# Split weight tiles kept in DRAM, and a depthwise convolution as diagonal matrix products

## The chip, the core and the metric

The kernel runs on one core of one Trainium2 chip. A core has five engines that run side by side, each from its own queue in order: TensorE (matrix products, "PE" in the profile, with "PEld" for loading its stationary operand), VectorE ("DVE"), ScalarE ("ACT"), GpSimd ("POOL") and SyncE ("SP", which here only issues transfers). Transfers between DRAM and on-chip memory run on 16 DMA engines. The metric is the device time of one execution in microseconds (us). Before the change it is 3492.43 us, the median of three runs (3483.12 to 3494.14).

## What is computed

The reference is one layer of a streaming encoder over 1024 tokens of 1024 channels in float32. Cut to what matters here:

```python
h = adaln(x, shift1, scale1)                  # layer norm, shifted and scaled by the condition c
p = h @ w_in                                  # 1024 -> 2816 columns
p_conv, p_rw = p[..., :1024], p[..., 1024:]

u = p_conv[..., :512] * sigmoid(p_conv[..., 512:])
u = causal_depthwise_conv(u, conv_w) + conv_b # 31 taps, one filter for each of 512 channels
y_conv = silu(layer_norm(u, conv_ln_g, conv_ln_b))

y_rw = rwkv7(p_rw)                            # recurrence over tokens, 8 heads of 64
y1 = concat([y_conv, y_rw]) @ w_out
x = layer_norm(ALPHA * x + gate1 * y1)

h2 = adaln(x, shift2, scale2)
q = h2 @ peer_wq                              # 1024 -> 2048 columns
# q against 2 x 128 keys for each of 8 heads, top 16, softmax -> 16 experts and gates for each head
# each of 16384 experts: gelu(h2 . u_e) * gate * v_e, summed over the chosen ones
return layer_norm(ALPHA * x + gate2 * y2)
```

## The kernel before

The kernel has a front end and a dense stage. The front end covers everything up to the choice of experts. The dense stage then runs all 16384 experts for 640 of the 1024 tokens as matrix products on TensorE, while the other 384 tokens gather their experts' rows by GpSimd transfers and use VectorE. The change lies in the front end alone.

Large products are made of float32 operands split in two: a high part in the reduced type float32r (`hi`) and the remainder (`lo`), so that a product is three float32r matmuls (hi x hi, hi x lo, lo x hi). `load_split` (L158) does this for a tile of weights, 128 contraction rows x 8 x 128 columns, 0.5 MB: it loads it raw by SP (L155, tile `wraw`, three buffers), ScalarE copies it to `whi` (L161), GpSimd subtracts to make `wlo` (L163), two buffers each. `proj` (L166) then issues 24 matmuls (L173) into one bank of the PSUM pool `psum`, whose tag `mm` (L145) has three buffers. Tiles of the 22 of `w_in` are loaded for each half of the tokens, the 8 of `w_out` and the 16 of `wq` for each of four blocks of 256 tokens: 44 + 32 + 64 = 140 calls.

The tokens go through in two halves of 512:

- `inproj(0)` (L262) runs first and alone: norm, transposition to channels, the condition's matrix-vector products on VectorE (`cond_some`, L234), all `w_in` tiles, and the streams for the recurrence, which it stores in DRAM (`AR_d`, `BK_d`, `v_d`, `bv_d`, `gt_d`). Its `glu` (L323) fills `ubuf`, 4 groups of 128 channels x (30 + 512) tokens, and appends `conv(0)` to the list `slow`.
- The recurrence follows in 16 chunks of 64 tokens: `solve` (L576) inverts each chunk's triangular system by a chain of small TensorE products and VectorE steps, `pass_state` (L654) carries the state. Between their matmuls `fill` (L553) is called, some 80 times for each chunk. It takes steps of the generators in `side` (`inproj(1)`, then `post` for each block of 256 tokens) and at every fourth call one step of the first generator in `slow` (the convolution, then `choose` and `gate_matrix`).
- `conv` (L436) handles 4 groups of 128 channels. In each, 18 taps are accumulated on VectorE in `cacc` (L443, L449), 13 on ScalarE and GpSimd: ScalarE scales a window into `ctap` (L453), GpSimd adds it to `cpool` (L454), and VectorE adds both sums (L457). Then come two sums over the channels by a matrix of ones (L460, L468) and the norm. `inproj(1)` drains `conv(0)` before its own `glu` overwrites `ubuf`, and the main loop drains `conv(1)` before chunk 8.
- `post` (L734): `w_out`, residual and norm, transposition, `wq`, keys and top 16. `choose` (L834) picks the 16 of 16 x 16 candidates, `gate_matrix` (L909) builds for each token block the matrix of gates over all experts out of one-hot tiles (`oa` L928, `ob` L932 to L944, products L946, `stage` L947) and stores it in DRAM as `G_d` (L949), 2 MB at a time from one buffer.

Semaphores and the order on each engine are made by the scheduler of the framework, which takes the order of the program's text as priority and moves an instruction ahead where its own model of time finds an engine free. Each engine then runs its queue in the order so fixed.

Of the kernel before, what the change touches and what calls it, by code (L numbers as in the profile page):

```python
# [10 lines left out]
F32 = mybir.dt.float32  # L11
F32R = mybir.dt.float32r
# [3 lines left out]
AF = mybir.ActivationFunctionType  # L16
OP = mybir.AluOpType
# [6 lines left out]
KD = 8  # L24
CW = 512
KS = 31
# [24 lines left out]
PSG, PSD = 3, 3  # L51
SLOW = 4
NTMP = 28
WRAW = 3
RUN = 4
STEPS = 4, 3
RATES = 1.0, 2.0
# [21 lines left out]
def layer_kernel(ctx, tc, x, cols, c_row, cond_w, w_in, w2a2, g2, w_out, ln_rows, wq, keys, peer_u, peer_ut, peer_v, peer_vt, out):  # L79
    nc = tc.nc  # L80
    V, A, G, T = nc.vector, nc.scalar, nc.gpsimd, nc.tensor
    ld = nc.sync.dma_start
# [3 lines left out]
    dram = ctx.enter_context(tc.tile_pool(name="dram", bufs=1, space=DRAM))  # L86
# [5 lines left out]
    def col(n, i=None):  # L92
        a, b = COFF[n]
        return colt[:, a:b] if i is None else colt[:, a + i:a + i + 1]
# [5 lines left out]
    ident = const.tile([128, 128], F32)  # L100
# [28 lines left out]
    h2_d = dt([128, D], "h2_d", 8)  # L129
    h2t_d = dram.tile([2, KD, 128, ND], F32, name="h2t_d")  # L130
    sel_d = dt([3, 128, 128], "sel_d", 8)
    G_d = dram.tile([32, 128, ND // TB, 4 * TB], F32, name="G_d")


# [2 lines left out]
    ws = fex.enter_context(tc.tile_pool(name="ws", bufs=2))  # L137
# [6 lines left out]
    def mm(w=512):  # L144
        return psum.tile([128, 512], F32, tag="mm", name="mm")[:, :w]  # L145
# [4 lines left out]
    def page(name, dt=F32, w=512):  # L150
        return pgp.tile([128, max(w, 512)], dt, tag="pg", name=name)[:, :w]

    def load_raw(src):
        raw = ws.tile([128, KD, 128], F32, name="wraw", bufs=WRAW)
        ld(raw, src)  # L155
        return raw

    def load_split(src):  # L158
        raw = load_raw(src)
        hi = ws.tile([128, KD, 128], F32R, name="whi")  # L160
        A.activation(hi, raw, AF.Copy)  # L161
        lo = ws.tile([128, KD, 128], F32R, name="wlo")
        G.tensor_sub(lo, raw, hi.bitcast(F32))  # L163
        return hi, lo

    def proj(w, act, pt):  # L166
# [95 lines left out]
    def inproj(h, ps, pg_):  # L262
# [10 lines left out]
        hi = [page("hhi", F32R) for _ in range(KD)]  # L273
        lo = [page("hlo", F32R) for _ in range(KD)]
        shift, scale = lambda k: mod[:, k:k + 1], lambda k: modp[:, k, 0:1]
        first = []
        if h == 0:

            for i in range(4):
                parts = load_x(i, tp)  # L280
                normalize(parts, parts)
                xn.append(parts)
            two = [(load_split(w_in[j]), mm()) for j in (0, 4)]
            for k in range(KD):
                cond_some((k, 8 + k), pg_)
                V.tensor_scalar_add(modp[:, k, 0:1], mod[:, 8 + k:9 + k], 1.0)
                to_channels(xn, shift, scale, hi, lo, None, (k,), m2)
                for (whi, wlo), pt in two:
                    for q, (l, r) in enumerate(((whi, hi), (whi, lo), (wlo, hi))):
                        T.matmul(pt, l[:, k, :], r[k], start=k == 0 and q == 0, stop=k == KD - 1 and q == 2)  # L290
            first = [pt for _, pt in two]
            ld(w2a2_t, w2a2)
            ld(g2_t, g2)
        else:
            for g in range(2):
                xn = []
                for i in range(2):
                    parts = load_x(4 * h + 2 * g + i, tp)
                    normalize(parts, parts)
                    xn.append(parts)  # L300
                sl = slice(256 * g, 256 * g + 256)
                to_channels(xn, shift, scale, [t[:, sl] for t in hi], [t[:, sl] for t in lo])
                yield

        def tile_of(j):
            w = load_split(w_in[j])
            pt = mm()
            yield from proj(w, (hi, lo), pt)
            return pt
# [113 lines left out]
        if h == 1:  # L423
            yield from glu()
            V.tensor_scalar_add(modp[:, :, 1], mod[:, 32:40], 1.0)
            pt = mm(128)
# [4 lines left out]


    slow, gates, gb, conv_left, psg, tail = [], [], [], [], [], []
    POOL_TAPS = 13

    def conv(h):  # L436
        acc = []
        for ct in range(4):
            wk = lambda k: colt[:, COFF["conv_w"][0] + KS * ct + k:COFF["conv_w"][0] + KS * ct + k + 1]
            win = lambda k: ubuf[:, ct, k:k + HALF]  # L440
            a, b = page("cacc"), page("cpool")
            acc.append(a)
            V.tensor_scalar(a, win(0), wk(0), col("conv_b", ct), op0=OP.mult, op1=OP.add)  # L443
            A.activation(b, win(KS - POOL_TAPS), AF.Copy, scale=wk(KS - POOL_TAPS))
            i, j = 1, KS - POOL_TAPS + 1
            while i < KS - POOL_TAPS or j < KS:
                for _ in range(2):
                    if i < KS - POOL_TAPS:
                        V.scalar_tensor_tensor(a, win(i), wk(i), a, op0=OP.mult, op1=OP.add)  # L449
                        i += 1  # L450
                if j < KS:
                    f = page("ctap")
                    A.activation(f, win(j), AF.Copy, scale=wk(j))  # L453
                    G.tensor_add(b, b, f)  # L454
                    j += 1
                yield
            V.tensor_add(a, a, b)  # L457
        pmn = mm()
        for ct in range(4):
            T.matmul(pmn, ones_m, acc[ct], start=ct == 0, stop=ct == 3)  # L460
        for ct in range(4):
            V.tensor_sub(acc[ct], acc[ct], pmn)
        yield
        pv = mm()
        for ct in range(4):
            s2 = page("s2")
            A.activation(s2, acc[ct], AF.Square)
            T.matmul(pv, ones_m, s2, start=ct == 0, stop=ct == 3)  # L468
        rs = page("crs")
        A.activation(rs, pv, AF.Sqrt, bias=eps_ln)  # L470
        V.reciprocal(rs, rs)
        yield
        for ct in range(4):
            y = acc[ct]
            V.tensor_mul(y, y, rs)
            A.activation(y, y, AF.Identity, bias=col("cln_b", ct), scale=col("cln_g", ct))
            sc_ = page("csig")
            A.activation(sc_, y, AF.Sigmoid)
            G.tensor_mul(y, y, sc_)
            ld(conv_d[h][ct], y)  # L480
            yield
        conv_left.remove(h)
# [251 lines left out]
    def post(t0, vpage):  # L734

        n, nt, tile0 = PB, PB // 128, t0 // 128
        fetch = [tile0 + t in GT for t in range(nt)]
        hp, hi = duo("ychi", F32R)
        lp, lo = duo("yclo", F32R)
        for i in range(KD // 2):  # L740
            f = page("ycf").rearrange("p (a t) -> p a t", a=2)
            if i < 2:
                c = t0 % HALF
# [7 lines left out]
        yield  # L751
        y1 = duo("y1")[1]
        for j in range(KD):
            w = load_split(w_out[j])
            pt = mm(n)
            yield from proj(w, (hi, lo), pt)
            A.activation(y1[j], pt, AF.Copy, scale=mod[:, 16 + j:17 + j])
# [8 lines left out]
        for t in range(nt):  # L766
            xt = load_x(tile0 + t, page)
            for i in range(2):
                pt = mm()
# [17 lines left out]
        hi, lo = duo("h2hi", F32R)[1], duo("h2lo", F32R)[1]  # L787
# [13 lines left out]
        for g in range(4):  # L801
            kt = pgp.tile([128, 4, 128], F32, tag="pg", name="keys")
            ld(kt, keys[:, 4 * g:4 * g + 4, :])
            qt = []
            for m in range(4):
                w = load_split(wq[4 * g + m])
                pt = mm(n)
                yield from proj(w, (hi, lo), pt)
                if m % 2 == 0:
                    qp = page("qt").rearrange("p (a t) -> p a t", a=2)  # L810
                A.activation(qp[:, m % 2, :], pt, AF.Copy)
                qt.append(qp[:, m % 2, :])
            for t in range(nt):
                ps = mm()
                for m in range(4):
                    T.matmul(ps[:, 128 * m:128 * m + 128], qt[m][:, 128 * t:128 * t + 128], kt[:, m, :],
                             start=True, stop=True)
                s = page("s12")
                A.activation(s, ps, AF.Copy)
                for m in range(4):  # L820
                    vs, ix = val[t][:, 2 * g + m // 2, m % 2], idx[t][:, 2 * g + m // 2, m % 2]
                    sm = s[:, 128 * m:128 * m + 128]
                    V.max(vs[:, 0:8], sm)  # L823
                    V.max_index(ix[:, 0:8], vs[:, 0:8], sm)  # L824
                    V.match_replace(sm, vs[:, 0:8], sm, -3.0e38)  # L825
                    V.max(vs[:, 8:16], sm)  # L826
                    V.max_index(ix[:, 8:16], vs[:, 8:16], sm)  # L827
                    yield
# [129 lines left out]
    for c in range(16):  # L958
# [16 lines left out]
        if flight:  # L975
            f = flight.pop(0)
# [40 lines left out]
    def mg(w=512):  # L1017
        return psg[0].tile([128, 512], F32, tag="mgate", name="mg", bufs=PSG)[:, :w]
# [105 lines left out]
    for g in range(32):  # L1124
# [4 lines left out]
        for e in range(4):  # L1129
# [7 lines left out]
            for bs in NBLK:  # L1137
                p = mg(NW)
                i = 0
# [12 lines left out]
        if g == 31:  # L1152
            xts = []
            for t in range(ND // 128):
                xts.append(de.tile([128, D], F32, tag="uraw" if t < 2 else "uhi" if t < 4 else "ulo", name="xres",
                                   bufs=2))
# [6 lines left out]
        for i, (blocks, c) in enumerate((b_, c) for b_ in parts for c in range(4)):  # L1163
# [3 lines left out]
            for d in range(2):  # L1167
                ds = slice(128 * d, 128 * d + 128)
                k = 2 * c + d
                for bs in blocks:  # L1170
                    p = md(bs.stop - bs.start)
# [10 lines left out]
            if g == 31 and c == 3:  # L1182
                for t in range(blocks[0].start // 128, blocks[0].stop // 128):
                    xt = xts[t]
                    for i_ in range(2):
                        pt = mg()
# [55 lines left out]
```

## Time and profile before

| what | us |
|---|---|
| median of three runs | 3492.43 |
| the profiled execution | 3490.03 |
| its span, first to last instruction | 3488.3 |
| TensorE busy | 3082.5 (88%) |
| VectorE busy | 2782.5 (80%) |
| GpSimd busy | 2134.7 (61%) |
| ScalarE busy | 1368.9 (39%) |

The page cuts the span in 40 slices of 87.2 us; a digit is the busy share of an engine in tenths (9 is 90% or more), and PEclk is the clock that TensorE was granted, in tenths of full speed. A table by stretch gives for each engine the busy time and, in brackets, the number of instructions, then the granted clock, the share of the DMA engines and GB/s. A group's row gives line, engine, operation, out<-in by the program's names, shapes and count, then busy time, the mean of one in ns, and the idle time of the engine before it with what ended it. A row by tile gives the shortest, median and longest of one in ns and the first and last start. PE instructions overlap in their pipeline, so the sum of their durations is more than the time they take together. A float32 matmul shows as two instructions, a float32r one as one; the profile writes f32 for both types.

### The profile page before, as it was taken

What the parts mean: (1) busy time and instruction counts of PE and PEld (TensorE: products, weight loads), DVE (VectorE), ACT (ScalarE), POOL (GpSimd) and SP (SyncE); (2) the same over time, 40 slices, a digit from 0 to 9 for tenths busy, and PEclk for the clock granted to TensorE, in tenths of its full rate; (3) what the DMA queues carried; (4) which work ended last, traced back from release to release, by engine and by line L of the source; (5) the groups of instructions that cost most, each with busy time, mean ns of one, the idle gap of its engine ahead of it and who ended that gap; (6) DMA issues with size and microseconds to landing.
All of it is one profiled execution on the core that took longest, in us unless ns stands there. A gap on an engine that the chain in (4) does not pass through costs nothing.

```text
span 3488.3 us, 59487 instructions
## 1 busy us (share of the span) xinstructions
PE 3082.5 (88%) x22536; PEld 2874.0 (82%) x22536; DVE 2782.5 (80%) x5776; ACT 1368.9 (39%) x2581; POOL 2134.7 (61%) x1522
## 2 busy tenths in 40 slices
PE   6965898888888766676999999999999999999997
PEld 4734566677787666576999999999999999999997
DVE  5399786897786799799777788877788877778887
ACT  4563444444554635764322222232222232222223
POOL 2446325474545366262677777687777777777773
PEclk9977788678798887787999999999999999999998
DMA  5434364333455544455799898999999989989894
GB/s 213 126 104 139 90 182 139 109 99 98 126 158 159 175 146 129 139 151 159 258 338 338 327 345 322 348 327 338 332 334 333 336 315 349 343 327 343 319 342 174
DMA packets 392223, 822.46 MB, mean 236 GB/s; under 512 B 76496, under 2 KB 209792, under 8 KB 387840
## 3 DMA queue, kind: packets, MB, share of 16 engines
q1 hardware_dynamic: 199104, 374.02, 32.5%
q0 software_dynamic: 110592, 402.70, 30.8%
q10 hardware_dynamic: 82240, 41.94, 4.3%
q8 instruction: 177, 2.90, 0.3%
q14 instruction: 110, 0.90, 0.1%
HBM read 738.84 MB, written 79.72 MB: 235 GB/s over the span
## 4 chain that ended last, share of the span: by engine, by line
PE 55%; DVE 12%; DMA 4%; ACT 2%; issue 1%; POOL 0%; SPq 0%; ACTq 0%; DVEq 0%; POOLq 0%
PE md L1175 25%; PE mg L1142 25%; DMA G_d<-stage 3%; DVE oa L928 2%; DVE ob L940 2%; PE mgate L946 2%; PE mm L173 2%; DVE vi L824 1%; DVE s L825 1%; ACT stage L947 1%; DVE vi L823 0%; DVE vi L827 0%; DVE oh L886 0%; DVE cand L849 0%; DVE vi L826 0%
## 5 line engine op out<-in xcount | busy, mean ns | idle before, releaser
L1175 PE MATMUL md<-ah,vhi 128*128 128x320 f32 x2048 | 629.2, 310 | 16.4 <-ACT ah L1147 14.8
L1142 PE MATMUL mg<-h2h,uhi 128*128 128x320 f32 x2048 | 635.3, 310 | 1.1 <-DVE al L1148 1.1
L1142 PE MATMUL mg<-h2l,uhi 128*128 128x320 f32 x2048 | 634.7, 310 | 0.0
L1142 PE MATMUL mg<-h2h,ulo 128*128 128x320 f32 x2048 | 634.4, 310 | 0.0
L1175 PE MATMUL md<-al,vhi 128*128 128x320 f32 x2048 | 631.2, 309 | 0.0
L1175 PE MATMUL md<-ah,vlo 128*128 128x320 f32 x2048 | 629.5, 309 | 0.0
L163 POOL TENSOR_TENSOR wlo<-wraw,whi 128x1024 fp32r<-128x1024 f32 x140 | 347.9, 2488 | 375.5 <-ACT whi L161 357.0
L1081 DVE SCALAR_TENSOR_TENSOR gy<-grow,gz,gy 128x1024 f32<-128x1024 f32 x381 | 487.9, 1281 | 0.9
L1074 DVE SCALAR_TENSOR_TENSOR grow<-grow,gh 128x1024 f32<-128x1024 f32 x384 | 463.7, 1212 | 13.3 <-DMA grow<-peer_u,eid 8.0
L1066 POOL DMA_INDIRECT grow<-peer_u,eid x384 | 362.4, 944 | 147.0 <-issue 63.9
L1066 POOL DMA_INDIRECT grow<-peer_v,eid x384 | 361.4, 941 | 128.7 <-issue 59.1
L1108 POOL TENSOR_TENSOR vlo<-vraw,vhi 128x1024 fp32r<-128x1024 f32 x132 | 318.5, 2413 | 150.6 <-ACT vhi L1106 143.0
L1180 DVE SCALAR_TENSOR_TENSOR yacc<-md,mod,yacc 128x320 f32<-128x320 f32 x496 | 270.7, 549 | 169.9 <-PE md L1175 137.1
L1175 PEld LDWEIGHTS md<-ah,vhi 128*128 128x128 f32 x2048 | 383.6, 188 | 18.3 <-ACT ah L1147 15.9
L1142 PEld LDWEIGHTS mg<-h2h,uhi 128*128 128x128 f32 x2048 | 386.2, 189 | 1.5 <-DVE al L1148 1.5
L1142 PEld LDWEIGHTS mg<-h2l,uhi 128*128 128x128 f32 x2048 | 386.3, 189 | 0.0
L1142 PEld LDWEIGHTS mg<-h2h,ulo 128*128 128x128 f32 x2048 | 386.1, 189 | 0.0
L1175 PEld LDWEIGHTS md<-al,vhi 128*128 128x128 f32 x2048 | 384.2, 188 | 0.0
L1175 PEld LDWEIGHTS md<-ah,vlo 128*128 128x128 f32 x2048 | 383.7, 188 | 0.1
L1106 ACT ACTIVATE vhi<-vraw 128x1024 fp32r<-128x1024 f32 x132 | 139.9, 1060 | 610.3 <-PE md L1175 472.2
L1108 POOL TENSOR_TENSOR ulo<-uraw,uhi 128x1024 fp32r<-128x1024 f32 x128 | 311.2, 2432 | 55.8 <-ACT uhi L1106 49.1
L946 PE MATMUL mgate<-oa,ob 128*128 128x128 f32 x1280 | 226.6, 333 | 125.6 <-ACT stage L947 58.6
(357 smaller groups left out, 6690.3 us busy)
## 6 DMA issues: line engine op xcount, KB each, us to landing
vraw<-peer_vt SPq DMA_DIRECT2D x132, 512.0 KB
uraw<-peer_ut SPq DMA_DIRECT2D x128, 512.0 KB
G_d<-stage ACTq DMA_DIRECT2D x20, 2048.0 KB
gmat<-G_d SPq DMA_DIRECT2D x32, 1280.0 KB
wraw<-wq SPq DMA_DIRECT2D x64, 512.0 KB
cw<-cond_w SPq DMA_DIRECT2D x48, 512.0 KB
wraw<-w_in SPq DMA_DIRECT2D x44, 512.0 KB
wraw<-w_out SPq DMA_DIRECT2D x32, 512.0 KB
```

Source lines behind the costliest of these rows:

```text
L163: G.tensor_sub(lo, raw, hi.bitcast(F32))
L173: T.matmul(pt, l[:, k, :], r[k], start=i == 0, stop=i == 3 * KD - 1)
L928: V.tensor_tensor(oa, iota[:, None, :].to_broadcast([128, 4, 128]), i1[:, ts, None].to_broadcast([128, 4, 128]), op=OP.is_equal)
L946: T.matmul(pt[:, t, :], ob[:, t, :], oa[:, t, :], start=True, stop=True)
L1066: G.indirect_dma_start(out=r, out_offset=None, in_=peer_u if k < 128 else peer_v, in_offset=bass.IndirectOffsetOnAxis(ap=eid[:, k % 128:k ...
L1074: V.scalar_tensor_tensor(r, r, 1.0, ht, op0=OP.mult, op1=OP.mult, accum_out=z[:, i:i + 1])
L1081: V.scalar_tensor_tensor(y, r, z[:, i - 128:i - 127], y, op0=OP.mult, op1=OP.add)
L1106: A.activation(hi, raw, AF.Copy)
L1108: G.tensor_sub(lo, raw, hi.bitcast(F32))
L1142: T.matmul(p, l[:, k, :], r[k][:, bs], start=i == 0, stop=i == 3 * KD - 1)
L1175: T.matmul(p, l[:, e, ds], r[:, bs], start=e == 0 and q == 0, stop=e == 3 and q == 2)
L1180: V.scalar_tensor_tensor(ya, p, mod[:, 40 + k:41 + k], ya, op0=OP.mult, op1=OP.add)
```

## The change

`load_split` takes the tensor and the tile's number. The first time, it loads and splits as before, now into the two halves of one tile `wsplit` (three buffers), and stores both halves in DRAM, 1 MB, under the tensor's name and the number. Each later time it loads the stored pair, 1 MB by SP, and neither ScalarE nor GpSimd takes part. The raw tile has two buffers instead of three; the condition's tiles `cw` in the second half share them.

`conv` makes all 31 taps on TensorE. For each group of channels it takes one `mm` bank; for each four taps ScalarE scales the identity matrix by the tap's column of weights to a diagonal matrix of 128 x 128, four in one page, and TensorE multiplies them with the four windows of `ubuf`, accumulating in the bank, in plain float32. After the last tap ScalarE reads the bank with the bias into `cacc`. A group has 8 steps of `slow` where it had 12.

```diff
-WRAW = 3
+WRAW = 2
+WSPLIT = 3
...
+    split_d = {}
...
-    def load_split(src):
-        raw = load_raw(src)
-        hi = ws.tile([128, KD, 128], F32R, name="whi")
-        A.activation(hi, raw, AF.Copy)
-        lo = ws.tile([128, KD, 128], F32R, name="wlo")
-        G.tensor_sub(lo, raw, hi.bitcast(F32))
+    def load_split(src, j):
+
+        both = ws.tile([128, 2, KD, 128], F32R, name="wsplit", bufs=WSPLIT)
+        hi, lo = both[:, 0], both[:, 1]
+        key = src.tensor.name, j
+        if key in split_d:
+            ld(both.bitcast(F32), split_d[key])
+        else:
+            raw = load_raw(src[j])
+            A.activation(hi, raw, AF.Copy)
+            G.tensor_sub(lo, raw, hi.bitcast(F32))
+            split_d[key] = dram.tile([128, 2, KD, 128], F32, name=f"split_{key[0]}{j}")
+            ld(split_d[key], both.bitcast(F32))
         return hi, lo
...
-            two = [(load_split(w_in[j]), mm()) for j in (0, 4)]
+            two = [(load_split(w_in, j), mm()) for j in (0, 4)]
...
-    POOL_TAPS = 13
...
-            a, b = page("cacc"), page("cpool")
+
+            pt = mm()
+            for k0 in range(0, KS, 4):
+                n = min(4, KS - k0)
+                dg = page("ctap").rearrange("p (k c) -> p k c", k=4)
+                for k in range(n):
+                    A.activation(dg[:, k, :], ident, AF.Copy, scale=wk(k0 + k))
+                for k in range(n):
+                    T.matmul(pt, dg[:, k, :], win(k0 + k), start=k0 + k == 0, stop=k0 + k == KS - 1)
+                yield
+            a = page("cacc")
+            A.activation(a, pt, AF.Identity, bias=col("conv_b", ct))
             acc.append(a)
-            V.tensor_scalar(a, win(0), wk(0), col("conv_b", ct), op0=OP.mult, op1=OP.add)
-            A.activation(b, win(KS - POOL_TAPS), AF.Copy, scale=wk(KS - POOL_TAPS))
-            i, j = 1, KS - POOL_TAPS + 1
-            while i < KS - POOL_TAPS or j < KS:
-                for _ in range(2):
-                    if i < KS - POOL_TAPS:
-                        V.scalar_tensor_tensor(a, win(i), wk(i), a, op0=OP.mult, op1=OP.add)
-                        i += 1
-                if j < KS:
-                    f = page("ctap")
-                    A.activation(f, win(j), AF.Copy, scale=wk(j))
-                    G.tensor_add(b, b, f)
-                    j += 1
-                yield
-            V.tensor_add(a, a, b)
```

The other calls of `load_split` (in `tile_of`, and in `post` for `w_out` and `wq`) pass the tensor and the number in the same way.

More of the change, by code (lines that the diff above doesn't have):

```diff
@@ L305, in tile_of @@
         def tile_of(j):
-            w = load_split(w_in[j])
+            w = load_split(w_in, j)
             pt = mm()
@@ L753, in post @@
         for j in range(KD):
-            w = load_split(w_out[j])
+            w = load_split(w_out, j)
             pt = mm(n)
@@ L805, in post @@
             for m in range(4):
-                w = load_split(wq[4 * g + m])
+                w = load_split(wq, 4 * g + m)
                 pt = mm(n)
```

## The prediction

> **What bounds the kernel now.** I read the page's slices first, then the busy times by stretch, cut where the program changes its work.
>
> ```profile
> PE   6965898888888766676999999999999999999997
> DVE  5399786897786799799777788877788877778887
> PEclk9977788678798887787999999999999999999998
> ...
> core 0: us, PE busy (x) PEld busy (x) DVE busy (x) ACT busy (x) POOL busy (x), PEclk, DMA share, GB/s
> 0.00:215.00 215.00, 161.22 (x624) 116.17 (x625) 114.02 (x217) 119.39 (x205) 68.03 (x39) 0.90 0.49 158
> 87.20:174.40 87.20, 87.20 (x364) 66.62 (x363) 31.80 (x25) 46.49 (x86) 36.92 (x16) 1.00 0.43 126
> 215.00:391.00 176.00, 117.08 (x737) 82.81 (x735) 170.46 (x223) 78.96 (x149) 109.10 (x62) 0.75 0.36 107
> 391.00:572.00 181.00, 169.10 (x1602) 123.95 (x1603) 129.72 (x222) 82.19 (x146) 54.00 (x30) 0.89 0.57 166
> 436.00:523.20 87.20, 79.98 (x797) 58.92 (x799) 71.40 (x122) 36.94 (x67) 23.38 (x12) 0.86 0.63 182
> 572.00:825.00 253.00, 207.56 (x2174) 177.75 (x2171) 211.36 (x452) 116.25 (x217) 155.58 (x90) 0.78 0.34 102
> 825.00:1150.00 325.00, 282.39 (x2930) 253.41 (x2929) 248.33 (x851) 168.56 (x367) 157.05 (x106) 0.84 0.44 133
> 1150.00:1640.00 490.00, 335.60 (x2195) 314.24 (x2192) 444.36 (x1418) 290.91 (x676) 240.11 (x170) 0.80 0.49 149
> 1640.00:3488.30 1848.30, 1809.57 (x12292) 1805.69 (x12290) 1464.23 (x2399) 512.62 (x827) 1350.84 (x1027) 0.99 0.88 323
> ```
>
> From 1640 on TensorE is busy 1810 of 1848 us: the dense expert stage, which the edit doesn't touch and whose length I keep. The edit lives before 1640. There TensorE is full only in the first projection (87 to 174); from 215 to 391, where the first half's convolution runs, VectorE is busy 170 of 176 us and TensorE 117, at a granted clock of 0.75. The second half's convolution lies in 572 to 825, VectorE 211 and TensorE 208 of 253. Behind 1150 VectorE carries 444 of 490.
>
> **The convolution: what goes.**
>
> ```profile
> L449 DVE SCALAR_TENSOR_TENSOR cacc<-u,colt,cacc x136: 630/1214/2884, 224.1 to 776.6; 128x512 f32<-128x512 f32 x136
> ...
> L443 DVE TENSOR_SCALAR cacc<-u,colt x8: 536/1010/1625, 219.8 to 735.5; 128x512 f32<-128x512 f32 x8
> L457 DVE TENSOR_TENSOR cacc<-cacc,cpool x8: 679/685/965, 274.9 to 778.6; 128x512 f32<-128x512 f32 x8
> ...
> L454 POOL TENSOR_TENSOR cpool<-cpool,ctap 128x512 f32<-128x512 f32 x96 | 153.4, 1606 | 28.3 <-ACT ctap L453 25.2
> ...
> L449 DVE SCALAR_TENSOR_TENSOR cacc<-u,colt,cacc 128x512 f32<-128x512 f32 x136 | 174.5, 1291 | 1.2
> ...
> L453 ACT ACTIVATE ctap<-u,colt 128x512 f32<-128x512 f32 x96 | 62.5, 712 | 1.5 <-POOL cpool L454 1.2 <-DVE cacc L457 0.2
> ```
>
> VectorE loses 174.5 + 8 x 1.0 + 8 x 0.7 = 188 us, 94 in each of the two stretches; GpSimd loses 153, ScalarE (96 + 8) x 0.71 = 74. VectorE then stands near 76 of 176 and 117 of 253 and bounds neither.
>
> **What comes: 248 tap matmuls, 124 in each half,** fp32, 128x128 on 128x512. The trace has that form elsewhere, as two instructions each:
>
> ```profile
> 111.23 0.39 PE L173 MATMUL mm<-hlo,whi 128*128 128x512 f32 x1
> 111.45 1.02 PE L369 MATMUL m<-sg,g_t 128*128 128x512 f32 x2
> 111.91 0.80 PE L173 MATMUL mm<-hhi,wlo 128*128 128x512 f32 x1
> 112.55 0.40 PE L173 MATMUL mm<-hhi,whi 128*128 128x512 f32 x1
> ...
> 749.83 1.98 PE L460 MATMUL mm<-cacc,ones_m 128*128 128x512 f32 x4
> ```
>
> Projection matmuls (float32r) start about 0.23 apart. Between 111.45 and 112.55 lie one fp32 matmul and one of those: 1.10 - 0.23 = 0.87 us at full clock. The four instructions of L460, two matmuls, took 1.98, some of it at a lower clock: at most 0.99 each. I take 0.87: 124 x 0.87 = 108 us for each half, 216 in all, and put the clock in separately.
>
> Can the two stretches hold it? Busy time times granted clock is about what the present work needs at full clock: 117.1 x 0.75 = 88 and 207.6 x 0.78 = 162. With 108 each: 196 against a stretch of 176, 270 against 253. So TensorE becomes the bound in both, and even at full clock with no idle the two cost 20 + 17 = **+37 us**; busy time also counts the tails of short bursts, so +20 is the lower end. With the clock (0.86) and busy share (92%) of the best mixed stretch, 436 to 523, it is 196 / 0.79 = 248 and 270 / 0.79 = 342: **+161**, the upper end. The truth lies between that row and 87 to 174 (full, 1.00): the taps come four at a time, 3.5 us without a gap, and their waits on VectorE shrink. I take 0.96 busy at 0.96 clock: 213 and 293, +37 and +40, together **+77**. The recurrence's matmuls queue behind these bursts in program order and VectorE waits for them, so this falls on the path.
>
> Weighing a rule: granted clock rises with busy share in the rows above (0.75 at 67%, 0.86 at 92%, 1.00 at 100%). The Trainium skill, "TensorE: Matmul & The Clock Gate", Part 1, says that the gate knows only half and full rate and opens after some 3.4 us of sustained activity. By it four-tap bursts would hold it open, and the two stretches would cost about 20 to 37 instead of 77; the rows are means over open and shut windows and don't contradict it. It is a rival below.
>
> ScalarE builds each tap's diagonal from a 128x128 tile.
>
> ```profile
> L943 ACT ACTIVATE ob<-iota,selneg x240: 384/393/428, 915.5 to 1628.4; 128x128 f32<-128x128 f32 x120
> ...
> L319 ACT ACTIVATE xm<-mm,nmu 128x512 f32<-128x512 f32 x14 | 9.4, 676 | 0.5 <-POOL cpool L454 0.5
> ...
> L316 ACT ACTIVATE pshift<-mm 128x512 f32<-128x512 f32 x14 | 8.2, 583 | 0.0
> ```
>
> 248 x 0.39 = 97 us replace 74: 1.6 us for four beside their 3.5 on TensorE, with ScalarE under half busy there. I cost it at 0; bare, it would be the 23 us of difference. The accumulation holds one of three `mm` banks for 27 us; the side work keeps two, one filling and one read out, also 0, with up to +18 (the 14 tiles of that time, each by its two readings of 0.68 and 0.58 us) if the third was needed.
>
> **The weights.** 140 tiles are split now; 46 stay (22 of `w_in`, 8 of `w_out`, 16 of `wq`), 94 come back ready split.
>
> ```profile
> L161 ACT ACTIVATE whi<-wraw x140: 1039/1057/1077, 12.7 to 1579.0; 128x1024 fp32r<-128x1024 f32 x140
> L163 POOL TENSOR_TENSOR wlo<-wraw,whi x140: 2332/2392/3248, 13.8 to 1580.2; 128x1024 fp32r<-128x1024 f32 x140
> ...
> L163 POOL TENSOR_TENSOR wlo<-wraw,whi 128x1024 fp32r<-128x1024 f32 x73 | 176.8, 2425 | 116.4 <-ACT whi L161 112.9 <-PE bank L719 3.4
> ...
> by line: DMA G_d<-stage 12.8%; DVE oa L928 11.4%; DVE ob L940 10.2%; PE mgate L946 8.6%; PE mm L173 8.3%; DVE vi L824 3.1%; DVE s L825 2.8%; ACT stage L947 2.8%; issue 2.6%; DVE vi L823 2.3%; DVE vi L827 2.2%; DVE cand L849 2.1%; DVE vi L82
> ...
> L928 DVE TENSOR_TENSOR oa<-iota,selt x160: 630/686/2822, 918.8 to 1630.5; 128x512 f32<-128x512 f32 x160
> ...
> L940 DVE TENSOR_SCALAR ob<-iota,selt x240: 327/339/2506, 919.4 to 1631.4; 128x128 f32<-128x128 f32 x120
> ...
> L940 DVE TENSOR_SCALAR ob<-iota,selt 128x128 f32<-128x128 f32 x240 | 141.9, 631 | 0.0
> ...
> L928 DVE TENSOR_TENSOR oa<-iota,selt 128x512 f32<-128x512 f32 x160 | 154.7, 967 | 51.3 <-PE mgate L946 45.4 <-ACT selt L919 5.6
> ...
> ACT whi L161 <- PE mm L173: 40.5, 14, 11.6
> ...
> PE mm L173 <- POOL wlo L163: 7.8, 7, 2.7
> ```
>
> 94 x 1.06 = 99 us leave ScalarE and 94 x 2.45 = 230 leave GpSimd. Neither bounds a stretch; the gain is in what they hold up. In the chain of waits from 889 to 1640 (751 us) `oa` and `ob` have 11.4 and 10.2%, 86 and 77 us. Medians are 0.686 and 0.339, means 0.967 and 0.631, with single ones stretched by 2.2 us, about one GpSimd instruction. Unstretched the chain would lose 86 x (1 - 0.686/0.967) = 25 and 77 x (1 - 0.339/0.631) = 36, 61 us. `wlo` is 177 of GpSimd's 397 us from 825 to 1640 (45%), and its long instructions stretch most: 27 to 61, I take 42. Add 8 for other VectorE steps of the chain, 10 for TensorE's waits on `wlo` and `whi`, and 5 (0 to 25) for ScalarE, whose queue stood 40 us at `whi` for a buffer. Against it 72 tiles load 1 MB instead of 0.5, 46 GB/s on some 140; `G_d` writes hold 12.8%, 96 us of the chain; a tenth more is +10. Together **-55**, between -10 and -95. What ends last then: those writes and TensorE's `mgate`.
>
> Between 391 and 572 nine `w_in` tiles need no split: **-5**.
>
> In the first 215 us 22 writes of 1 MB are new, on SP's queue behind `wlo`, the next raw loads and the `v_d`, `AR_d` stores behind them, with two raw buffers instead of three. At 158 GB/s for a share of 0.49 the engines' full rate is 322 GB/s: 23 MB take 72 us, the share goes to 0.82. A tile's split chain (1.06 + 2.4 us) and its transfers must fit the 5.5 us of its 24 matmuls, and TensorE is full from 87 to 174, so any lateness counts: 0 to +25, I take **+8**, near 0 as the engines keep room.
>
> **The sum:** 77 - 55 - 5 + 8 = +25 us on the profiled execution's 3490.0 (span 3488.3), 2.4 below the median of 3492.4: **3516**.
>
> **The rivals.** (a) *The gate stays open:* the taps run at full clock without idle, +20, and the later stretches give -65: 3445. For it: TensorE was granted 1.00 where it was full. Against it: no mixed stretch passed 0.89. The sign turns where the two stretches cost less than 52 us (55 + 5 - 8), that is where TensorE's 196 + 270 us of work take under 481. (b) *The bursts starve the recurrence:* busy share and clock stay near the 436 row's, 0.92 x 0.88: 242 and 333 us, +146, with -40 later and +15 at the start: 3606. For it: one program-ordered queue, ScalarE's diagonals late behind its own waits. Against it: VectorE, the partner, is half idle. (c) *The taps slide behind 825,* where TensorE needs 282 x 0.84 = 237 of 325 us: half the 77 vanishes, 3478. Against it: the gate stage's buffers wait for the convolution's. (d) That tiles are not reused can't be: 46 keys, each filled once.
>
> **How the numbers follow.** Likeliest 0.45 (its own range 3490 to 3555), (a) 0.27, (b) 0.20, (c) 0.08. A change under 0.3% (10 us) can't be told from none. Faster: (a), half of (c), a little of the likeliest: 0.31; same 0.09; slower 0.60. The range 3440 to 3606 takes in (a) to (b) and the bounds +20 to +161 and -10 to -95 short of their corners.
>
> **What will show it.** Right: 496 tap instructions of about 0.43 us start to start; TensorE over 93% busy from 215 to about 430 and again in the second convolution, VectorE under 60% there; the first pass's state some 35 us later; 46 `wlo`; `oa` and `ob` means near 0.75 and 0.4. Wrong: a first stretch no longer than 185 us (then (a)), `oa` and `ob` unchanged (then the -55 falls), or TensorE waiting on `wlo` in the first 215.

## The result and the profile after

| | before | changed |
|---|---|---|
| median of 7 runs, us | 3491.55 (3483.12 to 3496.77) | 3509.84 (3495.5 to 3512.2) |
| profiled span, us | 3488.3 | 3508.8 |

The ratio is 1.0051, with a 95% interval from 1.0036 to 1.0066: half a per cent slower, with an interval that stays above 1. Forecast were 3516 us, slower.

The slices of the page after, and the same stretches as before the change (us; busy time and number of instructions of TensorE, its weight loads, VectorE, ScalarE and GpSimd; granted clock, DMA share, GB/s):

```profile
PE   6979999999998886576899999999999999999997
DVE  5372363055767769778777888877788877778887
PEclk9979998979889888788899999999999999999998
...
0.00:215.00 215.00, 164.66 (x634) 118.60 (x635) 117.81 (x237) 120.93 (x214) 63.79 (x36) 0.90 0.84 294
215.00:391.00 176.00, 170.09 (x861) 92.33 (x859) 67.29 (x164) 62.28 (x179) 5.99 (x6) 0.98 0.46 139
391.00:572.00 181.00, 178.99 (x1653) 126.30 (x1652) 100.74 (x181) 84.40 (x159) 24.68 (x19) 0.99 0.55 166
572.00:825.00 253.00, 244.56 (x1668) 157.12 (x1667) 64.20 (x156) 92.81 (x234) 47.13 (x27) 0.88 0.38 126
825.00:1150.00 325.00, 293.49 (x3126) 266.30 (x3124) 230.17 (x988) 144.10 (x333) 97.57 (x81) 0.88 0.65 221
1150.00:1640.00 490.00, 340.91 (x2746) 322.69 (x2741) 387.70 (x1403) 268.66 (x676) 148.78 (x135) 0.81 0.61 202
```

The bound of the two convolution stretches has changed hands. From 215 to 391 TensorE went from 117 to 170 us busy of 176 and VectorE from 170 to 67; from 572 to 825 TensorE went to 245 of 253 and VectorE from 211 to 64. The number of TensorE instructions between 572 and 825 fell from 2174 to 1668: work that was done there now comes later. TensorE's clock there is 0.88, where the prediction took 0.96.

How late the recurrence is can be read from the write of its state, `SN`, once for each chunk (numbered from 0). These are timelines of VectorE (start, duration, line), first of the kernel before, for chunks 4, 5 and 9, then of the changed kernel:

```profile
571.75 0.42 DVE L673 TENSOR_TENSOR SN<-SN,bank 128x256 f32<-128x256 f32 x1
...
618.38 0.41 DVE L673 TENSOR_TENSOR SN<-SN,bank 128x256 f32<-128x256 f32 x1
...
824.72 0.42 DVE L673 TENSOR_TENSOR SN<-SN,bank 128x256 f32<-128x256 f32 x1
```

```profile
581.32 0.41 DVE L677 TENSOR_TENSOR SN<-SN,bank 128x256 f32<-128x256 f32 x1
...
704.55 0.42 DVE L677 TENSOR_TENSOR SN<-SN,bank 128x256 f32<-128x256 f32 x1 [0.69 <-ACT ctap L455]
...
901.51 0.40 DVE L677 TENSOR_TENSOR SN<-SN,bank 128x256 f32<-128x256 f32 x1
```

The changed kernel is 10 us late at chunk 4, 86 late at chunk 5 and 77 late at chunk 9. By the last copy of the gate stage, below for the kernel before and the changed one, only 16 us of it are left:

```profile
1637.80 0.60 ACT L947 ACTIVATE stage<-mgate 128x512 f32<-128x512 f32 x1 [3.10 <-PE mgate L946]
```

```profile
1654.08 0.58 ACT L951 ACTIVATE stage<-mgate 128x512 f32<-128x512 f32 x1
```

So some 70 us were lost in the stretch of the second half's convolution and some 60 were won back behind chunk 9. The rows by tile of the changed kernel (shortest, median, longest in ns), and the rows of the groups, show the parts of the change at work:

```profile
L457 PE MATMUL mm<-u,ctap x496: 590/592/1220, 216.6 to 807.2; 128*128 128x512 f32 x166
L455 ACT ACTIVATE ctap<-ident,colt x248: 385/390/416, 213.4 to 781.0; 128x128 f32<-128x128 f32 x124
...
L170 POOL TENSOR_TENSOR wsplit<-wraw,wsplit x46: 2342/2393/3081, 13.5 to 877.1; 128x1024 fp32r<-128x1024 f32 x46
...
L932 DVE TENSOR_TENSOR oa<-iota,selt 128x512 f32<-128x512 f32 x160 | 121.3, 758 | 97.5 <-PE mgate L950 93.6 <-ACT selt L923 3.7
L944 DVE TENSOR_SCALAR ob<-iota,selt 128x128 f32<-128x128 f32 x240 | 96.8, 443 | 0.0
```

496 instructions make the 248 taps, 46 tiles are split instead of 140, and the means of `oa` and `ob` fell from 967 and 631 ns to 758 and 443. The chain of waits from 889 to 1655 and the waits at the stage buffer (in the last fence those of the kernel before) show what took VectorE's place there:

```profile
by line: DMA G_d<-stage 22.5%; PE mm L182 17.2%; PE mgate L950 14.0%; DVE oa L932 3.3%; issue 3.1%; DMA wsplit<-split_wq 2.9%; ACT stage L951 2.8%; DVE ob L944 2.6%; DMA wsplit<-split_w_out 1.9%; PE mm L820 1.8%; PE bank L627 1.5%; ACT ob L
...
1265.62 20.62 DMA G_d<-stage
...
  DMA G_d<-stage: 108.4, 16
...
DMA to landing us min/median/max: 8.7/13.6/22.2
```

```profile
  DMA G_d<-stage: 40.0, 13
```

`oa` and `ob` hold 5.9% of 766 us, 45, where they held 163. The write of `G_d` holds 22.5%, 172 us, where it held 96, and ScalarE stood 108 us (40 before) waiting for its one stage buffer: the next gates can't be staged until the 2 MB are out. TensorE's matrix products grew in this chain as well: `mm` holds 17.2%, 132 us, where it held 62, and `mgate` 14.0%, 107 us, where it held 65. The shares of a chain always fill its window, so they say what was waited for, not what a part of the change is worth.

### The profile page after: what moved, and what is told of

It reads as the page before. It is cut to its first block, busy times and chain, and to the rows that moved or that the text cites. A ratio compares the mean times of both kernels' runs of the same rounds, so it can differ in the third digit from the quotient of the medians.

```text
span 3508.8 us, 60171 instructions
## 1 busy us (share of the span) xinstructions
PE 3212.3 (92%) x23032; PEld 2898.9 (83%) x23032; DVE 2456.2 (70%) x5624; ACT 1296.1 (37%) x2640; POOL 1743.1 (50%) x1332
## 3 DMA queue, kind: packets, MB, share of 16 engines
q10 hardware_dynamic: 82240, 41.94, 4.2%
## 4 chain that ended last, share of the span: by engine, by line
PE 78%; DVE 9%; DMA 8%; ACT 3%; issue 1%; POOL 1%; SPq 0%; ACTq 0%; DVEq 0%; POOLq 0%
PE md L1179 25%; PE mg L1146 25%; PE mm L182 12%; PE mm L457 6%; DMA G_d<-stage 5%; PE mgate L950 3%; PE bank L627 1%; DMA cw<-cond_w 1%; PE bank L596 1%; PE bank L647 1%; DVE cw L248 1%; DVE oa L932 1%; DMA wsplit<-split_wq 1%; ACT stage L951 1%; DVE ob L944 1%
## 5 line engine op out<-in xcount | busy, mean ns | idle before, releaser
L950 PE MATMUL mgate<-oa,ob 128*128 128x128 f32 x1280 | 214.1, 321 | 131.1 <-ACT stage L951 99.1
L950 PEld LDWEIGHTS mgate<-oa,ob 128*128 128x128 f32 x1280 | 192.3, 230 | 141.9 <-ACT stage L951 92.2
```

The costliest lines, as they stand in the source:

```text
L950: T.matmul(pt[:, t, :], ob[:, t, :], oa[:, t, :], start=True, stop=True)
```

## The experiments

Ratios are to the kernel before, run on the same chip; chunks and `SN` as above. The state tells where the recurrence stands, not how much of the other work is done by then.

| kernel | median us | ratio, 95% interval | `SN` of chunk 4 | of chunk 9 |
|---|---|---|---|---|
| before | 3489 to 3492 | 1 | 572 | 825 |
| changed | 3509.8 | 1.0051, 1.0036 to 1.0066 | 581 | 902 |
| weights alone | 3423.8 | 0.9802, 0.9776 to 0.9828 | 556 | 771 |
| taps alone | 3543.9 | 1.0150, 1.0129 to 1.0171 | 598 | 910 |
| weights, taps in the first half | 3459.2 | 0.9910, 0.9888 to 0.9932 | 580 | 791 |
| changed, two taps a step | 3498.7 | 1.0025, 1.0003 to 1.0047 | 600 | 953 |
| weights, 13 + 13 taps on TensorE | 3366.9 | 0.9662, 0.9632 to 0.9692 | 510 | 772 |
| weights, 12 + 6 taps | 3382.4 | 0.9699, 0.9670 to 0.9728 | 526 | 778 |
| weights, 16 + 16 taps | 3381.1 | 0.9678, 0.9653 to 0.9704 | 531 | 789 |
| changed, small pools | 3548.2 | 1.0175, 1.0142 to 1.0209 | 599 | 894 |
| the same, two stage buffers | 3471.8 | 0.9955, 0.9942 to 0.9968 | 603 | 896 |
| 13 + 13 taps, two stage buffers | 3325.6 | 0.9526, 0.9502 to 0.9550 | 531 | 785 |

### The two parts by themselves

First the weights alone: the changed kernel with the old convolution.

```diff
-            pt = mm()
-            for k0 in range(0, KS, 4):
...
+            a, b = page("cacc"), page("cpool")
+            acc.append(a)
+            V.tensor_scalar(a, win(0), wk(0), col("conv_b", ct), op0=OP.mult, op1=OP.add)
...
```

> The weights' part alone, convolution as before. Theory (the loss at chunk 9 is the second half's taps on TensorE, the later gain is the weights'): the state of chunk 9 is written near 825 us as before (changed kernel 901), oa and ob means near 0.75 and 0.40 us, G_d still lands slowly (13 us median), and the whole takes 3435 us (3410 to 3465). Rival (the loss lies in the weights' stores and the two raw buffers, the gain in GpSimd being rid of the taps): chunk 9 near 900, whole 3540 to 3580.

Then the taps alone: the kernel before with the new `conv`, and its old `load_split`.

> The taps' part alone, weights as before. Theory: chunk 9 near 900 us, oa and ob means 0.97 and 0.63 as before, G_d lands in about 10 us, whole 3565 us (3535 to 3595). Rival (the weights' part makes the loss): chunk 9 near 825, whole 3420 to 3460.

Both whole times lie in the theory's ranges and far from the rival's. The weights alone took 3423.8 us, 66 less than before; the taps alone 3543.9, 54 more. The state of chunk 9 stands at 771 us with the weights alone, well ahead of before, and at 910 with the taps alone, later than in the changed kernel: the loss at that point is the taps'. The rest of the theory held in part. I had expected 825 for chunk 9 with the weights alone and their gain behind it; the weights' part already gains 53 us by then. Behind it, up to the last stage copy, the weights alone save 26 us (787 where it was 813) and the taps alone 35 (778), so the 60 us that the changed kernel wins back there aren't the weights' alone. `oa` and `ob` are 760 and 452 ns with the weights alone. With the taps alone `ob` is 627, as before, so its relief is the weights'; `oa` is 862, so half of its fall from 967 comes with the taps alone too. `G_d` lands in 11.1 us (median) with the weights alone, where 13 was expected. These are the groups of both, and the landing of `G_d` in the kernel with the weights alone and in the one with the taps alone:

```profile
L938 DVE TENSOR_TENSOR oa<-iota,selt 128x512 f32<-128x512 f32 x160 | 121.7, 760 | 77.6 <-PE mgate L956 75.9 <-ACT selt L929 1.5
L950 DVE TENSOR_SCALAR ob<-iota,selt 128x128 f32<-128x128 f32 x240 | 98.9, 452 | 0.0
...
  DMA G_d<-stage: 58.5, 13
...
DMA to landing us min/median/max: 8.7/11.1/21.0
```

```profile
L935 DVE TENSOR_SCALAR ob<-iota,selt 128x128 f32<-128x128 f32 x240 | 141.4, 627 | 0.0
L923 DVE TENSOR_TENSOR oa<-iota,selt 128x512 f32<-128x512 f32 x160 | 137.9, 862 | 37.9 <-PE mgate L941 31.6 <-ACT selt L914 6.0
...
  DMA G_d<-stage: 39.5, 12
...
DMA to landing us min/median/max: 8.6/10.0/15.6
```

What stretches VectorE's instructions can be counted in the trace of the kernel before. Of its 160 `oa` the 90 that overlap no GpSimd instruction take 680 ns on average and at most 694, though ScalarE runs beside 73 of them; the 70 others take 1336. The taps in `cacc` behave the same: 738 ns (at most 752) for the 37 without GpSimd beside them, 1498 for the 99 others.

With 0.5 MB loads a `G_d` write took at most 15.6 us; with the 1 MB loads it took up to 21 and 22. In the changed kernel the nine writes beside which no weight load was under way landed in 8.7 to 11.7 us, the seven beside three or more of them in 17.0 to 22.2. It isn't these loads alone: one write of 18.7 us had a single one of them beside it, and 13 other transfers.

Added up, -66 and +54 make -12, and together they made +18. The 30 us between lie where both meet: the changed kernel waits 108 us for `G_d`, the parts 58 and 40. That this wait is the whole of the 30 us is argued, not shown; a second stage buffer was tried neither with the weights alone nor with the kernel before. Seen from the weights alone, all taps cost 86 us; added to the kernel before, 54.

### Which half pays

The changed kernel with the new taps for `h == 0` and the old convolution for `h == 1`:

```diff
+            if h == 0:
+                pt = mm()
...
+            else:
+                a, b = page("cacc"), page("cpool")
...
```

> Weights as changed, taps on TensorE in the first half only, second half's convolution as before. Theory (only the second half's taps delay the recurrence, since there TensorE also has the first post block's products): chunk 9 near 830 us, whole 3440 us (3415 to 3470), as the weights alone or a few us better. Rival (each half's TensorE work costs alike, as predicted at 37 and 40): whole 3475 (3465 to 3490).

Neither number came: 3459.2 lies between, below the rival's range and inside the theory's, which was wide. The theory's point fails all the same, and chunk 9 came at 791 instead of 830: against the weights alone the first half's taps cost 35 us, so they aren't free as I had come to think from the changed kernel's early states. From there to the changed kernel the second half's taps cost 51. By the intervals of the ratios each of the two is uncertain by some 10 us. The two prices that the prediction had given, 37 and 40, are closer than the theory I had formed after the result. What had misled me is that chunk 4 is only 10 us late in the changed kernel: the weights' part makes it 16 early (556 instead of 572), the taps 25 late.

### The order of the taps

Two taps in a step of `conv` instead of four:

```diff
-            for k0 in range(0, KS, 4):
-                n = min(4, KS - k0)
+            for k0 in range(0, KS, 2):
+                n = min(2, KS - k0)
```

> The changed kernel with two taps in a step of the convolution instead of four, so its matmuls are spread over twice as many steps. Theory A (the order costs: tap bursts and post products ahead of the recurrence's chain): chunk 5's state, 704 us in the changed kernel and 618 before, comes back to 640 to 670, whole 3470 to 3495. Theory B (TensorE's work costs wherever it stands, 108 us more in a stretch that has 45 idle): whole 3500 to 3520.

3498.7 us falls between the two. Chunk 5 came at 684 instead of 704, far from 618, and chunk 9 at 953, 51 us later than in the changed kernel. The gain of some 11 us is hardly clear of the noise, since the intervals of the two ratios overlap. It is no clean verdict, but most of the 86 us stays with the taps spread as well. What delays chunk 5 shows in the changed kernel's busy times around it (columns as above) and TensorE's groups from 600 to 720:

```profile
600.00:720.00 120.00, 120.00 (x592) 66.54 (x593) 9.09 (x22) 36.67 (x102) 17.13 (x8) 0.98 0.32 109
720.00:780.00 60.00, 53.32 (x624) 43.08 (x622) 35.72 (x100) 34.79 (x86) 10.58 (x8) 0.66 0.44 133
...
740.00:760.00 20.00, 17.09 (x173) 13.63 (x169) 13.60 (x36) 7.11 (x15) 2.53 (x2) 0.50 0.27 89
...
L457 PE MATMUL mm<-u,ctap 128*128 128x512 f32 x186 | 88.8, 609 | 0.0
L182 PE MATMUL mm<-ychi,wsplit 128*128 128x256 f32 x116 | 31.3, 345 | 0.0
L182 PE MATMUL mm<-yclo,wsplit 128*128 128x256 f32 x58 | 20.4, 352 | 0.0
```

For 120 us TensorE is never idle, at 0.98 of the clock, and does taps and the first post block's `w_out` products; the recurrence gets what is left, and VectorE, its partner, is busy 9 us. From 720 to 760 no tap runs, and TensorE does the recurrence's small products and some of the post block's work; its clock drops, to 0.50 from 740 to 760, though it is busy 17 of those 20 us. The work hasn't only grown, it has lost the mixture that kept both engines going; how much of the loss is due to that, no run separates. In the kernel with smaller pools, further below, chunk 5 comes at 610 and chunk 6 at 733: there the jump falls one chunk later.

### Taps shared between the engines

If a stretch lasts as long as its fullest engine, VectorE's 18 taps should stay, and only the 13 of ScalarE and GpSimd go to TensorE:

```diff
+    PE_TAPS = 13, 13
...
+            k0 = KS - PE_TAPS[h]
+            i, j = 1, k0
+            while i < k0 or j < KS:
+                for _ in range(2):
+                    if i < k0:
+                        V.scalar_tensor_tensor(a, win(i), wk(i), a, op0=OP.mult, op1=OP.add)
+                        i += 1
+                n = min(2, KS - j)
+                if n:
...
+                        T.matmul(pt, dg[:, k, :], win(j + k), start=j + k == k0, stop=j + k == KS - 1)
+                    j += n
+                yield
+            V.tensor_add(a, a, pt)
```

> Weights as changed; of the 31 taps, 18 stay on VectorE and the 13 that were ScalarE's and GpSimd's go to TensorE, in both halves. Theory (a convolution's stretch lasts as long as its fullest engine needs): first half TensorE 88 + 45 us, VectorE about 130, of 176 with the weights alone; second half TensorE 162 + 45, VectorE about 155, of 253; 20 to 25 us less in each, whole 3380 us (3355 to 3400). Rival (tap matmuls delay the recurrence by their order on TensorE, whatever room it has): 42% of the 86 us that all taps cost beside the changed weights, 3424 + 36 = 3460.

> The same with 12 taps on TensorE in the first half and 6 in the second, the rest on VectorE, none on GpSimd. Theory: second half TensorE 162 + 21 us and VectorE about 174, so its stretch falls most, whole 3360 us (3340 to 3385), below the kernel with 13 and 13. Rival (order): 29% of 86, 3449.

> The kernel with 13 and 13, but 16 taps on TensorE and 15 on VectorE. By the fullest engine: second half TensorE 162 + 56 us at a clock near 0.87 is 250 of its 253 us, VectorE no longer last: whole 3375 us (3365 to 3395), no better than 13 and 13. If VectorE still bounds there: 3345 to 3360.

With 13 and 13 it is 3366.9 us, 57 under the weights alone (49 by the ratios), within the theory's range; the rival's +36 is out. With 16 and 16 it is 3381.1, in the expected range, though the intervals of these two overlap. But 12 and 6 came at 3382.4 and not below 3366.9: taps moved back to VectorE in the second half cost more than I had counted; VectorE was busy 205 us from 572 to 825, where I had 174. The rows of VectorE's taps of the kernel before stand in the prediction (mean 1291 ns); these are the kernel with 12 and 6, then the one with 13 and 13:

```profile
L460 DVE SCALAR_TENSOR_TENSOR cacc<-u,colt,cacc 128x512 f32<-128x512 f32 x168 | 151.1, 910 | 1.7
```

```profile
L460 DVE SCALAR_TENSOR_TENSOR cacc<-u,colt,cacc 128x512 f32<-128x512 f32 x136 | 113.3, 844 | 1.8
...
215.00:391.00 176.00, 167.27 (x1063) 106.89 (x1062) 142.35 (x276) 70.92 (x163) 16.90 (x12) 0.97 0.65 204
391.00:572.00 181.00, 170.99 (x1771) 125.23 (x1770) 117.31 (x207) 73.40 (x150) 35.59 (x23) 0.96 0.53 165
572.00:825.00 253.00, 236.70 (x2479) 194.57 (x2476) 181.41 (x612) 104.20 (x223) 86.34 (x59) 0.87 0.64 218
```

A VectorE tap takes 844 to 910 ns with GpSimd rid of the convolution; I had worked with 740, about what a tap takes with no GpSimd instruction beside it, and in the kernel with 13 and 13 20 of the 136 taps still overlap one. VectorE's 18 taps didn't move in this kernel; they became shorter, 113 us in all where they are 162 with the weights alone, where 85 of the 136 overlap a GpSimd instruction. In the kernel with 13 and 13 both engines are well filled from 215 to 391 (167 and 142 us of 176), where the kernel before had 117 and 170 and the changed one 170 and 67. Its lead over the weights alone is 46 us at chunk 4, nothing at chunk 9 and 54 at the last stage copy, so the theory's 20 to 25 us for each half can't be read from the recurrence.

### The wait on G_d

A second stage buffer needs 16 KB, so this pair has fewer pages and fewer `oa` and `ob` buffers; the first is the control.

```diff
-NPAGE = 35
+NPAGE = 30
...
-GB = 3
+GB = 2
...
-            stage = gb[0].tile([128, 128, TB], F32, name="stage", bufs=1)
+            stage = gb[0].tile([128, 128, TB], F32, name="stage", bufs=2)
```

> The changed kernel with 30 pages instead of 35 and two buffers of oa and ob instead of three, which makes room for the next kernel and is its control. Every theory: as the changed kernel or slower, 3505 to 3540 us; G_d lands in 13 us (median).

> Its control plus a second stage buffer, so that the next 32 tokens' gates are built while G_d is written. Theory (the 1 MB loads stretch the G_d writes to 20 us, and that wait gave back most of what the weights' part gained on VectorE): ScalarE's 108 us of waits on G_d fall under 30, whole 40 to 80 us below its control. Rival (the gate steps are bound by VectorE, ScalarE and TensorE anyway): within 15 us of its control.

The control took 3548.2 us, 38 more than the changed kernel and 8 above the stated range. The second buffer took 76 off it, within the expected 40 to 80, to 3471.8; the rival is out. These are the waits of ScalarE at the stage buffer, the control's first, then those with two stage buffers, in which `G_d` no longer appears:

```profile
  DMA G_d<-stage: 56.4, 15
```

```profile
its engine sat idle before it (us, times) until:
  PE mgate L950: 125.3, 82
who waited for it (us, times):
  PEld mgate L950: 21.3, 18
  PE mgate L950: 19.4, 21
```

So with one buffer that write set the pace of the gate stage. But in the control ScalarE waited only 56 us for it, not the 108 of the changed kernel, although the control is the slower one: the length of this wait alone doesn't give the price. In the profiles 59 of the second buffer's gain lie before the last stage copy (1687.3 and 1628.2 us) and 15 behind it, in the dense stage, where the cause is open. Nor do the runs show how much of the gain is due to the 1 MB loads: ScalarE waited 40 us for this write before the change too.

Last, both finds together: 13 and 13 taps with the second buffer and the small pools.

> Weights as changed, 13 taps on TensorE and 18 on VectorE in both halves, and the second stage buffer with 30 pages and two buffers of oa and ob. If the gains add: 3367 + 38 (small pools, from the control) - 76 (second buffer) = 3329 us (3315 to 3350). If the wait on G_d was long only because all taps delayed the gate stage into the weight loads: 3365 to 3400.

They add: 3325.6 us, where 3329 were expected (the rival from 3365 is out), 4.7% under the kernel before and 5.2% under the changed one.

## Why the prediction was right, point by point

**The sum.** +25 us were forecast on the profiled execution; the span grew by 20.5 and the median by 18. (The sum makes 3515 for the profiled execution and 3517 for the median; 3516 is neither.) That it came so near is partly luck. Measured alone, the taps cost 54 where the sum has 77, and the weights gain 66 where it has 52: the two added up would make the kernel 12 us faster. What made it slower is the 30 us by which the two together exceed that, for which the sum had only the +10 of the `G_d` writes. Counted in the other order, the weights first and the taps beside them, the prices are -66 and +86, and the terms are 14 and 9 off.

**The taps' price.** 0.87 us for one, two instructions. In the changed kernel 16 instructions in a row took 7.14 us:

```profile
621.59 7.14 PE L457 MATMUL mm<-u,ctap 128*128 128x512 f32 x16
```

(7.14 - 0.59) / 15 = 0.437 for an instruction, 0.87 for a tap. Right, and so was the price of a diagonal, 0.39 us on ScalarE, which cost nothing that shows: TensorE waited 6 us for `ctap` in all.

**The two stretches, +37 and +40.** Measured as differences of whole kernels, beside the new weights, they are 35 and 51. That TensorE becomes the bound of both was right (97% busy, where over 93% was asked). The clock was better than the 0.96 I took in the first stretch (0.98) and from 600 to 720, among the taps (0.98), but 0.88 over the whole second one. What failed is where I said that the loss would be seen: I wanted the first pass's state 35 us later, and it came 6 us earlier; by the sign I had set for it, rival (a) would have won. The loss sat at chunk 5 and after. Rival (b), bursts that starve the recurrence, is what the second stretch looks like from 600 to 720, though at a full clock and not at 0.88; the low clock, 0.66 from 720 to 780, comes after. I had weighed that the clock rises with the busy share: there TensorE is busy 89% at 0.66, where the row from 436 to 523 of the kernel before has 92% at 0.86, so it doesn't follow the share. The trace's records of the clock hold only 1.00 and 0.50, in stretches that are, but for one, multiples of 3.4 us; in the changed kernel it is 1.00 from 604.6 to 734.3 us and 0.50 from there to 775.2. The Trainium skill, "TensorE: Matmul & The Clock Gate", Part 1, which knows half and full rate alone and lets the gate open after some 3.4 us of activity, fits that. Full clock didn't make the taps free, since the stretch was full of work and not of slow clock.

**The weights, -55 - 5 + 8.** Alone they gave -66 for -52, so the size was nearly right. Its inside was mis-sized: in the chain `oa` and `ob` hold 118 us less, where I took 42 (bound 61), and the write of `G_d` 76 more, where I took 10; `mm` and `mgate` hold 112 more, for which I had nothing. By busy time `oa` and `ob` lost 33 and 45 us. I had counted the 46 GB/s more in the mean; the writes meet the loads in bursts. The size came near although its inside was wrong.

The Trainium skill, "DMA: Bandwidth & Descriptors", Queues, rings and completion order, says that each DMA engine takes turns between the queues at the grain of a packet. `G_d` is issued on ScalarE's queue and the weight loads on SP's; that a write took 17.0 to 22.2 us beside three or more loads and 8.7 to 11.7 beside none fits this. The page of the changed kernel has 82240 packets and 41.94 MB for the queue of `G_d`, 510 bytes for one on average. No run here changed the packet size, so what it costs isn't shown.

```profile
q10 hardware_dynamic: 82240, 41.94, 4.2%
```

**The start, +8.** Nothing that shows: the first tap starts at 216.6 us, the first convolution instruction before at 219.8. The DMA share rose to 0.84 (0.82 was worked out), and the first projection bore it.

**Chances.** The likeliest case was the right one: TensorE became the bound of both stretches, and the weights gave back most of what the taps cost. That the total was met within 7 us owes something to chance, since the terms inside the sum were off by up to 76.

## What to carry to other kernels

Moving work off a full engine gains only up to where the next engine is full: count what the receiving engine needs at full clock in that very stretch, and if it doesn't fit, move a part. Here 13 of 31 taps on TensorE were worth 57 us, all 31 cost 86; the 13 were not VectorE's own but those that GpSimd had added beside it. An operation on one engine that stretches another's (here GpSimd's instructions and VectorE's compares and taps) is worth more than its own time shows, and when it goes, look for the next wait on the same chain: the wait for a buffer that is written out by DMA can be lengthened by just the loads that replace the computing.

## What the runs showed that I had not expected

In the changed kernel a `G_d` write of 2 MB took 8.7 to 11.7 us beside no weight load and 17 to 22 beside three or more loads of 1 MB, though the DMA engines' share from 1150 to 1640 was only 0.61. Taking five of 35 pages and one of three gate buffers away cost 38 us, half of what the second stage buffer then gave. And a VectorE tap of 738 ns took 1498 on average where a GpSimd instruction overlapped it.
